# Down projection: activation sums made in the convolution and kept in HBM, 25 groups by seven

## The chip, the cores and the metric

One core of one Trainium2 chip runs the kernel. The metric is device time in microseconds; a lower number is better. The profile names the engines PE (matrix multiply), PEld (its weight loads), DVE (vector), ACT (scalar), POOL (GpSimd) and SP (which issues most DMAs).

## The reference

One transformer block on 256 tokens of width 2048: three attention branches with gates, then a gated feed-forward layer with a short convolution. The change concerns only its last lines (`D_FF` is 5632):

```python
h2 = rms_norm(x, g_ffn[l])
u = causal_depthwise_conv(h2 @ w_up[l], conv_w[l], conv_b[l])
u_gate, u_val = jnp.split(u, 2, axis=-1)
x = x + (jax.nn.silu(u_gate) * u_val) @ w_down[l]
```

## The kernel before

All products keep nearly float32 accuracy by splitting each operand into a high and a low part: ACT casts the raw tile to `hi`, DVE subtracts to get `lo`, and PE adds three products, high by high, low by high and high by low (`three`, lines 1309 to 1311). Of `hi` and `lo` there are four buffers each (`SBUFS`). A cast waits until PE has finished with what lay in the buffer four casts before.

**The up projection** (lines 1219 and 1221) streams 176 weight tiles of 128x1024. Its results go through `conv`, which DVE and ACT work off beside PE: scale, three taps, SiLU, product `g`, and the split of `g` into `aT`, the activations of the down projection, transposed, with high and low part. `conv` takes two feature slices of 128 at a time, 22 such pairs.

**The down projection** multiplies `aT` (44 slices of 128 features) by `w_down` in two halves `nb` of 1024 output columns. A group `p` is a pair of slices `k0 = 2p`, `k1 = 2p+1`, with two halves `t` of the tokens and two halves `n` of the columns: a 2x2 by 2x2 block product. `eight` does it in eight block products (24 matmuls of 128x512). `seven` does it in seven (21 matmuls), by a scheme of Strassen's kind: four of the seven use sums of the weights, `T1` to `T4`, and sums of the activations, `FS1` to `FS4` ("forms"). `PLANS` gives the order in each half; an "e" is a group by eight, an "s" a group by seven. Before, there are 8 and 14 sevens.

Where the sums come from, before:

- Weight sums: `weight_sums` runs during the up projection, one group every seven weight tiles. It loads the four blocks, adds on DVE and stores T4 and T2 to HBM by POOL's queue; for the 12 groups in `ALL_FOUR` it stores T1 and T3 too. In the other 10, `p2` of `seven` makes T1 and T3 by two additions on DVE (lines 1371 and 1372) into a tile of its own.
- Forms: `forms(p)` makes them during the down projection by five DVE instructions from `aT` (lines 1273 to 1277), then splits them by two casts on ACT (1281, 1282) and two subtractions on DVE (1284, 1285). Results lie in `sf` and in parts of `aT` no longer needed.

**What sets the order.** In the down projection the order on each engine is written out: `steps` holds pairs (preparation, use), an eight has two, a seven four (`p0`/`u0` to `p3`/`u3`, of 3, 6, 6 and 6 matmuls); the preparation of step i+2 is issued ahead of the use of step i (`AHEAD`), and `keep` pins it. `after_step` starts generators after a given step; `tick` advances each of at most four by one piece a step. In the trace each engine runs its instructions in that order. SP issues the loads of weights as their buffers (`raw`, `more`) come free. POOL's queue carries the stores of sums, the loads of the residual (`xr`) and half of the results. The tag `junk` has two buffers; `conv`'s scratch, `forms` and `gather` share them.

Of the kernel before, what the change touches and what calls it, by code (L numbers as in the profile page):

```python
# [15 lines left out]
P = 128  # L16
# [32 lines left out]
OUT_SEVENS = 3  # L49
NSEVEN = tuple(plan.count("s") for plan in PLANS)  # L50


@with_exitstack
def hybrid_block(
# [1075 lines left out]
    def conv(ps, f, s):  # L1130
# [20 lines left out]
        if s == 0:  # L1151
            nc.scalar.activation(y, y, AF.Silu)
            ys[f] = y
        else:
            g = ys.pop(f)
            nc.vector.tensor_tensor(g, g, y, ALU.mult)
# [7 lines left out]
            ended.append(f)  # L1164

    ended = []
    made = {}
    asked = [(0, p) for p in range(NSEVEN[0])] + [(1, p) for p in range(NSEVEN[1])]

    def weight_sums(nb, p):  # L1170
# [10 lines left out]
        add = lambda o, i: tc.keep_in_program_order(nc.vector.tensor_tensor(o, o, i, ALU.add))  # L1181
        four = (nb, p) in ALL_FOUR
        add(r[0][:, 0], r[0][:, 1])
        if four:
            add(r[0][:, 1], r[1][:, 1])
        yield 1
        add(r[1][:, 1], r[0][:, 0])
        add(r[1][:, 0], r[1][:, 1])
        made[nb, p] = [dram.tile([P, PIECE], F32, name=f"T{j}_{nb}_{p}") for j in range(1 + four)]
        if four:  # L1190
            nc.gpsimd.dma_start(made[nb, p][1], r[0].rearrange("p b n -> p (b n)"))
        yield 1
# [53 lines left out]
    ov = out[0].rearrange("(t p) d -> p t d", p=P)  # L1246
    FS3, FS1, FS2, FS4 = range(4)
# [8 lines left out]
    def form_of(p, f):  # L1256
        if f == FS4:
            return pieces_of(p)[:, 0, :, 1]
        if p < 10:
            return sf[:, p, f]  # L1260
        return pieces_at(31 - p).rearrange("p k (f l q) -> p (k f) l q", f=2, l=2)[:, f]

    def forms(p):

        flat = aT[:, 2 * p : 2 * p + 3].rearrange("p k s -> p (k s)").bitcast(F32)
        v = flat[:, :1024].rearrange("p (k l t q) -> p k l t q", k=2, l=2, t=NT)
        d = sm.tile([P, 512], F32, tag="junk", bufs=2, name=f"fd_{p}").rearrange("p (f l q) -> p f l q", f=2, l=2)
        r = down_pool().tile([P, 512], F32, tag="fr", bufs=1, name=f"fr_{p}").rearrange("p (f q) -> p f q", f=4)
        g = rbc.rearrange("p (k q) -> p k q", k=2)
        two = flat[:, : 2 * 640].rearrange("p (a b) -> p a b", b=640)[:, :, :512]  # L1270
        two = two.rearrange("p a (l t q) -> p a l t q", l=2, t=NT)[:, :, :, 0]
        tt = nc.vector.tensor_tensor
        keep(tt(d, two, v[:, 0, :, 1].unsqueeze(1).to_broadcast([P, 2, 2, P]), ALU.subtract))
        keep(tt(g, v[:, :, 0, 0], v[:, :, 1, 0], ALU.add))
        keep(tt(r[:, :2], d[:, :, 0], d[:, :, 1], ALU.add))
        keep(nc.vector.scalar_tensor_tensor(r[:, FS2], r[:, FS1], -1.0, g[:, 0], ALU.mult, ALU.subtract))
        keep(tt(r[:, FS4], r[:, FS2], g[:, 1], ALU.add))
        yield
        to = sf[:, p] if p < 10 else form_of(p, slice(0, 3))
        last = form_of(p, FS4)  # L1280
        keep(nc.scalar.copy(to[:, :, 0], r[:, :3]))
        keep(nc.scalar.copy(last[:, 0], r[:, FS4]))
        yield
        keep(tt(to[:, :, 1], r[:, :3], to[:, :, 0].bitcast(F32), ALU.subtract))
        keep(tt(last[:, 1], r[:, FS4], last[:, 0].bitcast(F32), ALU.subtract))

    turn = [0]

    def buffer(name):
        turn[0] += 1  # L1290
        if turn[0] > 10 and turn[0] % 3 == 0:
            return down_pool().tile([P, PIECE], F32, tag="more", bufs=2, name=name)
        return wp.tile([P, PIECE], F32, tag="raw", name=name)

    def load(src, name):
        raw = buffer(f"raw_{name}")
        keep(nc.sync.dma_start(raw[:, : src.shape[1]], src))
        return raw
# [51 lines left out]
    def seven(p, n0, X, Y, first, last):  # L1350
        k0, k1 = 2 * p, 2 * p + 1
        name = f"{n0}_{p}"
        w, raw = {}, {}
        four = (n0 // PIECE, p) in ALL_FOUR

        def p0():
            n = 512 if four else PIECE
            raw[0] = load(dv[:, k0, n0 : n0 + n], f"s{n0}_{k0}")
            (w["00"],) = parts(raw[0][:, :512], f"s{n0}_{k0}")

        def p1():
            raw[1] = load(dv[:, k1, n0 : n0 + PIECE], f"s{n0}_{k1}")
            w["10"], w["11"] = parts(raw[1], f"s{n0}_{k1}")

        def p2():
            raw[2] = load(made[n0 // PIECE, p][0], f"t{name}")
            raw[3] = down_pool().tile([P, PIECE], F32, tag="t13", bufs=2, name=f"t13_{name}")
            if four:
                keep(nc.sync.dma_start(raw[3], made[n0 // PIECE, p][1]))
            else:  # L1370
                keep(nc.vector.tensor_tensor(raw[3][:, :512], raw[0][:, :512], raw[0][:, 512:], ALU.add))
                keep(nc.vector.tensor_tensor(raw[3][:, 512:], raw[0][:, 512:], raw[1][:, 512:], ALU.add))
            w["T4"], w["T2"] = parts(raw[2], f"t42_{name}")

        def p3():
            w["T1"], w["T3"] = parts(raw[3], f"t13_{name}")

        def u0():
            three(Y()[0], *a_of(k0, 0), w["00"], first, last)

        def u1():
            three(X()[0][0], *a_of(k1, 0), w["10"])
            three(X()[0][1], *f_of(p, FS4), w["11"])
# [62 lines left out]

    formed = 0
    after_step = {}
# [4 lines left out]
    for nb, plan in enumerate(PLANS):  # L1453
# [5 lines left out]
        if nb == 0:  # L1459
            at(-1, lambda: start(0))  # L1460
        for i, c in enumerate(plan):
            if c == "s":
                seven(s, n0, X, Y, s == 0, s == ns - 1)
                s += 1
                if s == ns:
                    at(len(steps) - 1, lambda nb=nb: later(gather(nb, banks[nb][1])))
            else:
                eight(straight.pop(0), n0, X, i == 0, i == len(plan) - 1)
                n_done += 1
                if n_done == 4:  # L1470
                    at(len(steps) - 1, lambda nb=nb: residual(nb))
                if formed < ns and n_done >= 4 - 3 * nb:
                    at(len(steps) - 2, lambda p=formed: later(forms(p)))
                    formed += 1
        assert s == ns and not straight and formed >= ns
        at(len(steps) - 1, finish)
# [48 lines left out]
```

## Time and profile before

| | |
|---|---|
| three runs | 1472.62 us median, 1472.32 to 1474.24 |
| profiled execution, first to last instruction | 1469.9 us; the median run lies 2.7 us above it |
| down projection, first to last matmul | 1241.05 to 1465.25 us |
| DVE, ACT, POOL busy over the whole span | 82%, 61%, 5% |
| HBM read, written | 349.70 MB, 37.75 MB |

All times below are microseconds from the start of the span. In the rows of the trace a time stands first and a duration second where the row is one of the timeline; an engine's row in square brackets tells how long it sat idle before and what ended that. Instructions on DVE and ACT overlap a little at their ends, so a row's successor can start before it is over; costs in a row of back-to-back work go by start to start.

### The profile page before, as it was taken

The page shows a single profiled execution, that of the slowest core. Times are in us where ns is not written, and L with a number is a line of the kernel's source. Part 1 is how long each engine was busy: PE and PEld are TensorE (multiplying, and loading weights), DVE is VectorE, ACT ScalarE, POOL GpSimd, SP SyncE. Part 2 cuts the span into 40 slices and gives each one's busy share as a digit, 9 for nine tenths or more (in the row PEclk, how much of TensorE's full clock was granted, in tenths as well). Part 3 has the DMA queues.
Part 4 walks back from the last instruction along what each step waited for, and adds up shares of the span by engine and source line. Part 5 has one row for each costly group of instructions (what it writes and reads, how often), then busy time and mean ns, then how long its engine had stood idle before and what let it go on. Part 6 is the DMA issues. An engine that isn't in the chain of part 4 may idle for free.

```text
span 1469.9 us, 20741 instructions
## 1 busy us (share of the span) xinstructions
PE 1462.8 (100%) x7327; PEld 1233.4 (84%) x7327; DVE 1205.1 (82%) x1617; ACT 895.3 (61%) x1287; POOL 68.8 (5%) x139
## 2 busy tenths in 40 slices
PE   9999999999999999999999999999999999999998
PEld 7888888888878888888888888888888888888887
DVE  5798767766997799888877888788887886998998
ACT  6755454454664466545657667567676777665774
POOL 1000001021000000000000000000000010000000
PEclk9999999999999999999999999999999999999999
DMA  8697898787766576866776888889888895778995
GB/s 295 202 341 260 265 313 270 226 294 267 256 221 204 204 271 247 287 222 237 273 239 218 302 272 276 294 277 310 295 265 273 280 305 190 249 256 286 334 315 191
DMA packets 163463, 388.81 MB, mean 265 GB/s; under 512 B 14016, under 2 KB 22512, under 8 KB 163360
## 3 DMA queue, kind: packets, MB, share of 16 engines
q1 hardware_dynamic: 150960, 345.34, 70.6%
q0 software_dynamic: 11648, 41.10, 7.3%
q8 instruction: 57, 0.93, 0.3%
q10 hardware_dynamic: 752, 1.06, 0.2%
q14 instruction: 46, 0.38, 0.1%
HBM read 349.70 MB, written 37.75 MB: 264 GB/s over the span
## 4 chain that ended last, share of the span: by engine, by line
PE 94%; DVE 3%; DMA 2%; issue 1%; ACT 0%; SPq 0%; DVEq 0%; ACTq 0%
PE u L1219 21%; PE u L1221 10%; PE d L1310 5%; PE d L1309 5%; PE d L1311 5%; PE g_x L769 4%; PE g_x L770 4%; PE g_x L771 4%; PE s L186 2%; PE s L188 2%; PE f L187 2%; PE f L188 2%; PE f L186 2%; PE s L187 2%; PE b L186 2%; PE b L188 2%
## 5 line engine op out<-in xcount | busy, mean ns | idle before, releaser
L1219 PE MATMUL u<-hT,hi_u 128*128 128x512 f32 x1408 | 442.6, 396 | 0.0
L1221 PEld LDWEIGHTS u<-hT,lo_u 128*128 128x128 f32 x1408 | 264.4, 188 | 63.5 <-DVE lo_u L176 1.1
L1221 PE MATMUL u<-hT,lo_u 128*128 128x256 f32 x1408 | 277.0, 278 | 0.7 <-DVE lo_u L176 0.7
L176 DVE TENSOR_TENSOR lo_u<-raw_u,hi_u 128x1024 fp32r<-128x1024 f32 x176 | 213.2, 1220 | 59.8 <-ACT hi_u L175 59.0
L175 ACT CAST hi_u<-raw_u 128x1024 fp32r<-128x1024 f32 x176 | 183.0, 1049 | 107.0 <-PE u L1219 54.6
L1219 PEld LDWEIGHTS u<-hT,hi_u 128*128 128x128 f32 x1408 | 214.5, 189 | 0.1
L764 ACT CAST hi_g<-raw_g 128x1024 fp32r<-128x1024 f32 (+1 forms) x96 | 91.1, 964 | 53.5 <-PE g_x L770 33.4
L765 DVE TENSOR_TENSOR lo_g<-raw_g,hi_g 128x1024 fp32r<-128x1024 f32 (+1 forms) x96 | 105.0, 1116 | 20.9 <-ACT hi_g L764 20.8
L769 PE MATMUL g_x<-hi_g,xT 128*128 128x512 f32 x251 | 98.8, 394 | 0.0
L770 PE MATMUL g_x<-hi_g,xT 128*128 128x512 f32 x251 | 97.7, 389 | 0.0
L771 PE MATMUL g_x<-lo_g,xT 128*128 128x512 f32 x251 | 96.3, 390 | 0.0
L1148 DVE TENSOR_TENSOR y<-y,z 128x512 f32<-128x512 f32 x88 | 60.7, 691 | 24.4 <-ACT z L1147 20.5
L1147 ACT ACTIVATE z<-u,taps 128x256 f32<-128x256 f32 x176 | 74.7, 496 | 0.0
L1309 PE MATMUL d<-hi_d,aT 128*128 128x512 f32 x176 | 68.5, 389 | 0.0
L1310 PE MATMUL d<-hi_d,aT 128*128 128x512 f32 x176 | 68.5, 389 | 0.0
L1311 PE MATMUL d<-lo_d,aT 128*128 128x512 f32 x176 | 68.1, 389 | 0.0
L175 ACT CAST hi_f<-raw_f 128x1024 fp32r<-128x1024 f32 (+1 forms) x40 | 38.6, 968 | 46.6 <-PE f L187 41.9
L186 PE MATMUL s<-hi_s,xT 128*128 128x512 f32 (+1 forms) x160 | 61.9, 387 | 0.0
L175 ACT CAST hi_b<-raw_b 128x1024 fp32r<-128x1024 f32 x32 | 33.6, 1052 | 45.2 <-PE b L187 23.5
L175 ACT CAST hi_s<-raw_s 128x1024 fp32r<-128x1024 f32 (+1 forms) x40 | 38.3, 959 | 36.8 <-PE s L187 29.3
L186 PE MATMUL f<-hi_f,xT 128*128 128x512 f32 (+1 forms) x160 | 60.4, 377 | 0.0
L188 PE MATMUL s<-lo_s,xT 128*128 128x512 f32 (+1 forms) x160 | 59.1, 369 | 0.0
(498 smaller groups left out, 3265.0 us busy)
## 6 DMA issues: line engine op xcount, KB each, us to landing
raw_u<-in_w_up_dram SPq DMA_DIRECT2D x176, 512.0 KB, 5.4
raw_g<-in_w_in_dram SPq DMA_DIRECT2D x86, 512.0 KB, 5.4
T<-r POOLq DMA_DIRECT2D x64, 512.0 KB, 6.1
r<-in_w_down_dram SPq DMA_DIRECT2D x88, 256.0 KB, 5.2
raw_d<-in_w_down_dram SPq DMA_DIRECT2D x44, 512.0 KB, 5.4
raw_f<-in_w_in_dram SPq DMA_DIRECT2D x32, 512.0 KB, 5.5
raw_s<-in_w_in_dram SPq DMA_DIRECT2D x32, 512.0 KB, 5.4
raw_s<-in_w_down_dram SPq DMA_DIRECT2D x32, 512.0 KB, 5.3
```

The source lines that it names most:

```text
L175: pin(nc.scalar.copy(hi[:, :m], raw[:, :m]))
L176: pin(nc.vector.tensor_tensor(lo[:, :m], raw[:, :m], hi[:, :m].bitcast(F32), ALU.subtract))
L186: nc.tensor.matmul(o, lhsT=xh, rhs=wh, start=first, stop=False)
L188: nc.tensor.matmul(o, lhsT=xh, rhs=wl, start=False, stop=last)
L769: nc.tensor.matmul(o, lhsT=a[0], rhs=w[0], start=first, stop=False)
L770: nc.tensor.matmul(o, lhsT=a[1], rhs=w[0], start=False, stop=False)
L771: nc.tensor.matmul(o, lhsT=a[0], rhs=w[1], start=False, stop=last)
L1219: nc.tensor.matmul(ps, lhsT=hi[:, j, c], rhs=hT[:, k + j, :], start=first, stop=False)
L1221: nc.tensor.matmul(ps[:, :S], lhsT=lo[:, j, c], rhs=hT[:, k + j, :S], start=False, stop=last)
L1309: nc.tensor.matmul(o, lhsT=ah, rhs=w[0], start=first, stop=False)
L1310: nc.tensor.matmul(o, lhsT=al, rhs=w[0], start=False, stop=False)
L1311: nc.tensor.matmul(o, lhsT=ah, rhs=w[1], start=False, stop=last)
```

## The change

The unsplit forms (five additions' worth, now three instructions) are made at the end of `conv`, from `g`, for the first 15 pairs of slices, in the tile of `y`, and stored to HBM (`rform`) by POOL. `forms(p)` now loads them back by POOL's queue into a `junk` tile, waits three steps, and splits them as before. There are 25 sevens, 10 and 15. The eight groups in `OWN` have no weight sums in HBM: `p1` of `seven` makes all four by four additions on DVE, in place in the two raw tiles. The other 17 load all four sums from HBM. `weight_sums` is started every nine weight tiles. Of the buffers for raw weights, `more` has four and is used every second time; the tile for T1 and T3 is gone.

```diff
-PLANS = ("eeeee" + "se" * 5 + "sse" + "s" + "eee", "e" + "sse" * 4 + "ssse" + "sssee")
-ALL_FOUR = {(0, 6), (0, 7)} | {(1, p) for p in range(14) if p not in (4, 6, 8, 11)}
+PLANS = ("eee" + "sse" * 5 + "e" + "eee", "e" + "ssse" * 4 + "sss" + "ee")
+OWN = {(0, 1), (0, 3), (0, 5), (0, 7), (0, 9), (1, 3), (1, 7), (1, 11)}
...
+            if f // 2 < NFORM:
+                yield 1
+                unsplit_forms(f // 2, g, y)
...
+    def unsplit_forms(p, g, y):
+        v = g.rearrange("p k (t q) -> p (k t) q", t=NT)
+        r = y.rearrange("p k (t q) -> p (k t) q", t=NT)
+        tt = nc.vector.tensor_tensor
+        tt(r[:, :2], v[:, 0:4:3], v[:, 1:2].to_broadcast([P, 2, P]), ALU.subtract)
+        nc.vector.scalar_tensor_tensor(r[:, FS2], r[:, FS1], -1.0, v[:, 0], ALU.mult, ALU.subtract)
+        tt(r[:, FS4], r[:, FS2], v[:, 2], ALU.add)
+        rforms[p] = dram.tile([P, 512], F32, name=f"rform{p}")
+        nc.gpsimd.dma_start(rforms[p], y.rearrange("p k s -> p (k s)"))
...
-                if asked and n_ticks[0] > 8 and n_ticks[0] % 7 == 2:
+                if asked and n_ticks[0] > 8 and n_ticks[0] % 9 == 2:
...
     def forms(p):
...
+        r = sm.tile([P, 512], F32, tag="junk", bufs=2, name=f"fr_{p}").rearrange("p (f q) -> p f q", f=4)
+        keep(nc.gpsimd.dma_start(r.rearrange("p f q -> p (f q)"), rforms[p]))
+        yield 3
+        to, last = form_of(p, slice(0, 3)), form_of(p, FS4)
         keep(nc.scalar.copy(to[:, :, 0], r[:, :3]))
         keep(nc.scalar.copy(last[:, 0], r[:, FS4]))
         yield
...
-        if turn[0] > 10 and turn[0] % 3 == 0:
-            return down_pool().tile([P, PIECE], F32, tag="more", bufs=2, name=name)
+        if turn[0] > 10 and turn[0] % 2 == 0:
+            return down_pool().tile([P, PIECE], F32, tag="more", bufs=4, name=name)
...
         def p1():
             raw[1] = load(dv[:, k1, n0 : n0 + PIECE], f"s{n0}_{k1}")
             w["10"], w["11"] = parts(raw[1], f"s{n0}_{k1}")
+            if own:
+                add(raw[0][:, :512], raw[0][:, 512:])
+                add(raw[0][:, 512:], raw[1][:, 512:])
+                add(raw[1][:, 512:], raw[0][:, :512])
+                add(raw[1][:, :512], raw[1][:, 512:])
 
         def p2():
...
+            if not own:
+                raw[1] = load(made[n0 // PIECE, p][0], f"t{name}")
+                raw[0] = load(made[n0 // PIECE, p][1], f"t13_{name}")
+            w["T4"], w["T2"] = parts(raw[1], f"t42_{name}")
...
         if nb == 0:
             at(-1, lambda: start(0))
+            for p in range(10):
+                at(p + 1, lambda p=p: later(forms(p)))
         for i, c in enumerate(plan):
             if c == "s":
                 seven(s, n0, X, Y, s == 0, s == ns - 1)
+                if nb and s + 10 < NFORM:
+                    at(len(steps), lambda p=s + 10: later(forms(p)))
```

What the change moves stands best in the engines' own order. First ACT, at the first two groups by seven of the first half and the eight behind them. `hi_s` is the high part of a raw weight, `hi_t42` and `hi_t13` those of the weight sums, `hi_d` that of a weight of a group by eight, `sf` and `aT` from `fr_p` the two copies of form `p`. Before:

```order
L1304 CAST hi_s0_1_12062<-raw_s0_1_12060 128x1024
L1281 CAST sf_11814<-fr_1_12054 128x3x128
L1282 CAST aT_6836<-fr_1_12054 128x128
L1304 CAST hi_t42_0_0_12085<-raw_t0_0_12080 128x1024
L1304 CAST hi_t13_0_0_12094<-t13_0_0_12082 128x1024
L1304 CAST hi_d0_26_12106<-raw_d0_26_12104 128x1024
L1304 CAST hi_d0_27_12118<-raw_d0_27_12116 128x1024
```

In the change, from the second seven's first sum on (the first seven's stand above it):

```order
L1304 CAST hi_t42_0_1_12084<-raw_s0_3_12068 128x1024
L1280 CAST sf_11849<-fr_2_12031 128x3x128
L1281 CAST aT_6836<-fr_2_12031 128x128
L1280 CAST sf_11849<-fr_3_12033 128x3x128
L1281 CAST aT_6836<-fr_3_12033 128x128
L1304 CAST hi_t13_0_1_12095<-raw_s0_2_12049 128x1024
L1280 CAST sf_11849<-fr_4_12047 128x3x128
L1281 CAST aT_6836<-fr_4_12047 128x128
L1304 CAST hi_d0_26_12113<-raw_d0_26_12111 128x1024
L1280 CAST sf_11849<-fr_5_12061 128x3x128
L1281 CAST aT_6836<-fr_5_12061 128x128
L1304 CAST hi_d0_27_12133<-raw_d0_27_12131 128x1024
```

Before, one pair of copies stood in each seven; now pairs 2 to 5 stand between the casts of the second seven and of the eight behind it, pairs 6 and 7 likewise ahead of `hi_t13_0_2`, pair 8 ahead of `hi_s0_6` and pair 9 ahead of `hi_s0_7` of the fourth seven.

Next POOL, whose queue carries the loads of the forms; in brackets the semaphores that an issue waits for (DMASW are landings of earlier transfers of this queue). Before, no such load exists. Now:

```order
L1277 DMA fr_2_12031<-rform2_7878 128x512 [waits DMASW0_49,DMASW5_49,DVE_49,Activation_49]
L1404 DMA xr_0_1_1_12191<-xkeep1_6083 128x512 [waits DMASW6_49]
L1277 DMA fr_3_12033<-rform3_7883 128x512 [waits DMASW1_49,DMASW7_49,DVE_49,Activation_49]
L1277 DMA fr_4_12047<-rform4_8333 128x512 [waits DMASW5_49,DVE_49,Activation_49]
L1277 DMA fr_5_12061<-rform5_8338 128x512 [waits DMASW7_49,DVE_49,Activation_49]
L1277 DMA fr_6_12127<-rform6_8794 128x512 [waits DMASW0_49,DMASW2_49,DVE_49,Activation_49]
```

Each waits for DVE and ACT, since `junk` has two buffers: the load of form p+2 goes out once form p has been split.

Last DVE, in the second seven, a group of `OWN`. Before, a seven that makes T1 and T3 itself (the form's five instructions left out of these rows):

```order
L1305 TENSOR_TENSOR lo_s0_3_12156<-raw_s0_3_12153,hi_s0_3_12155 128x1024
L1371 TENSOR_TENSOR t13_0_1_12175<-raw_s0_2_12128 128x512
L1372 TENSOR_TENSOR t13_0_1_12175<-raw_s0_2_12128,raw_s0_3_12153 128x512
L1305 TENSOR_TENSOR lo_t42_0_1_12179<-raw_t0_1_12173,hi_t42_0_1_12178 128x1024
L1284 TENSOR_TENSOR sf_11814<-fr_2_12147,sf_11814 128x3x128
L1285 TENSOR_TENSOR aT_6836<-fr_2_12147,aT_6836 128x128
L1305 TENSOR_TENSOR lo_t13_0_1_12188<-t13_0_1_12175,hi_t13_0_1_12187 128x1024
```

In the change:

```order
L1305 TENSOR_TENSOR lo_s0_3_12071<-raw_s0_3_12068,hi_s0_3_12070 128x1024
L1355 TENSOR_TENSOR raw_s0_2_12049<-raw_s0_2_12049 128x512
L1355 TENSOR_TENSOR raw_s0_2_12049<-raw_s0_2_12049,raw_s0_3_12068 128x512
L1355 TENSOR_TENSOR raw_s0_3_12068<-raw_s0_3_12068,raw_s0_2_12049 128x512
L1355 TENSOR_TENSOR raw_s0_3_12068<-raw_s0_3_12068 128x512
L1305 TENSOR_TENSOR lo_t42_0_1_12085<-raw_s0_3_12068,hi_t42_0_1_12084 128x1024
L1305 TENSOR_TENSOR lo_t13_0_1_12096<-raw_s0_2_12049,hi_t13_0_1_12095 128x1024
L1283 TENSOR_TENSOR sf_11849<-fr_2_12031,sf_11849 128x3x128
L1284 TENSOR_TENSOR aT_6836<-fr_2_12031,aT_6836 128x128
```

`hi_t42` now reads `raw_s0_3`, so its cast stands behind the low part of the same tile and four additions; before, it read a tile that came from HBM.

More of the change, by code (lines that the diff above doesn't have):

```diff
@@ L1188, in weight_sums @@
         add(r[1][:, 0], r[1][:, 1])
-        made[nb, p] = [dram.tile([P, PIECE], F32, name=f"T{j}_{nb}_{p}") for j in range(1 + four)]
-        if four:
-            nc.gpsimd.dma_start(made[nb, p][1], r[0].rearrange("p b n -> p (b n)"))
+        made[nb, p] = [dram.tile([P, PIECE], F32, name=f"T{j}_{nb}_{p}") for j in range(2)]
+        nc.gpsimd.dma_start(made[nb, p][1], r[0].rearrange("p b n -> p (b n)"))
         yield 1
@@ L1353, in seven @@
         w, raw = {}, {}
-        four = (n0 // PIECE, p) in ALL_FOUR
+        own = (n0 // PIECE, p) in OWN
+        add = lambda o, i: keep(nc.vector.tensor_tensor(o, o, i, ALU.add))
         def p0():
-            n = 512 if four else PIECE
+            n = PIECE if own else 512
             raw[0] = load(dv[:, k0, n0 : n0 + n], f"s{n0}_{k0}")
@@ L1471, in hybrid_block @@
                     at(len(steps) - 1, lambda nb=nb: residual(nb))
[L1472 to L1475, printed above, removed]
+        assert s == ns and not straight
         at(len(steps) - 1, finish)
```

47 lines of the change are left out of this document (11 added, 36 removed).

## The prediction

> **What bounds the kernel now.** I read the page first, then the stages of the second half, then single instructions of the down projection.
>
> ```profile
> PE 1462.8 (100%) x7327; PEld 1233.4 (84%) x7327; DVE 1205.1 (82%) x1617; ACT 895.3 (61%) x1287; POOL 68.8 (5%) x139
> ```
>
> ```profile
> core 0: us, PE busy (x) PEld busy (x) DVE busy (x) ACT busy (x) POOL busy (x), PEclk, DMA share, GB/s
> 900.00:1000.00 100.00, 99.32 (x571) 86.36 (x570) 79.63 (x97) 66.51 (x101) 5.86 (x11) 1.00 0.87 288
> 1138.00:1241.00 103.00, 103.00 (x593) 89.86 (x593) 82.87 (x98) 72.77 (x113) 5.59 (x11) 1.00 0.82 269
> 1270.00:1305.00 35.00, 35.00 (x157) 28.97 (x156) 34.70 (x52) 22.35 (x28) 0.00 (x0) 1.00 0.75 260
> 1355.00:1412.00 57.00, 57.00 (x254) 47.19 (x253) 53.31 (x75) 38.60 (x47) 3.24 (x6) 1.00 0.92 322
> ```
>
> PE never rests in the down projection (the last two rows), and in the up projection (the two above) it lost 0.7 us in one stretch. DVE is at 34.7 of 35 us in one stretch and DMA at 0.92 in another. A busy PE need not be a PE at its pace, so I check that by counting:
>
> ```profile
> 1241.05 0.40 PE L1309 MATMUL d<-hi_d,aT 128*128 128x512 f32 x1
> ...
> 1465.25 0.39 PE L1311 MATMUL d<-lo_d,aT 128*128 128x512 f32 x1
> ```
>
> 22 sevens of 21 and 22 eights of 24 are 990 matmuls; 224.20 us over 989 steps are **0.2267 us** each, the spacing of neighbours too. So PE runs without a gap: every microsecond that a tile is late shows in the end.
>
> How late may a tile be? ACT's rows of two neighbouring sevens:
>
> ```profile
> 1426.28 0.62 ACT L1304 CAST hi_s<-raw_s 128x512 fp32r<-128x512 f32 x1
> 1427.37 1.05 ACT L1304 CAST hi_s<-raw_s 128x1024 fp32r<-128x1024 f32 x1 [0.47 <-PE d L1310]
> 1428.73 1.06 ACT L1304 CAST hi_t<-raw_t 128x1024 fp32r<-128x1024 f32 x1 [0.30 <-PE d L1310]
> 1430.09 1.05 ACT L1304 CAST hi_t<-t 128x1024 fp32r<-128x1024 f32 x1 [0.30 <-PE d L1310]
> ```
>
> The casts come at steps of 1.36 us (six matmuls), each released by PE: with four buffers ACT can't run further ahead. The second starts 0.10 us before the seven in front ends its second step; PE wants this seven's third tile 21 matmuls after that end, 4.86 us after the cast's start. The last, done at 1431.14, is wanted about 1433.6: **the lead is some 2.5 us**.
>
> **The change, part by part.**
>
> *Fewer products.* Three more sevens save 3 matmuls each: 9 x 0.2267 = **-2.0 us**, all on PE's path.
>
> *Up projection.* The 15 forms cost DVE three instructions each, by the rows of this kernel's own forms:
>
> ```profile
> 1274.33 0.42 DVE L1275 TENSOR_TENSOR fr<-fd 128x256 f32<-128x256 f32 x1
> 1274.78 0.29 DVE L1276 SCALAR_TENSOR_TENSOR fr<-fr,rbc 128x128 f32<-128x128 f32 x1
> 1275.11 0.29 DVE L1277 TENSOR_TENSOR fr<-fr,rbc 128x128 f32<-128x128 f32 x1
> ```
>
> That is 1.0 us, 15 in all; 17 groups of four additions instead of 12 of four and 10 of three save 10 x 0.6 = 6. The 9 us more lie beside PE, since DVE idles for a fifth of these stretches: I take 0. The stretch that lost 0.7 us bounds it: -0.7 if that goes, +1.4 if it doubles. The 15 stores on POOL hold only a `y` tile that isn't wanted for another 40 us.
>
> *Sums made in the seven itself.* DVE's rows for its pace, and an addition that needs the one before it:
>
> ```profile
> 1275.32 1.22 DVE L1305 TENSOR_TENSOR lo_s<-raw_s,hi_s 128x1024 fp32r<-128x1024 f32 x1
> 1276.45 0.68 DVE L1371 TENSOR_TENSOR t<-raw_s 128x512 f32<-128x512 f32 x1
> 1277.05 0.68 DVE L1372 TENSOR_TENSOR t<-raw_s,raw_s 128x512 f32<-128x512 f32 x1
> 1277.66 1.22 DVE L1305 TENSOR_TENSOR lo_t<-raw_t,hi_t 128x1024 fp32r<-128x1024 f32 x1
> ...
> 1457.39 0.68 DVE L1411 TENSOR_TENSOR e<-e,d 128x512 f32<-128x512 f32 x1
> 1458.11 0.69 DVE L1413 TENSOR_TENSOR f<-e,d 128x512 f32<-128x512 f32 x1
> ```
>
> Start to start, a low part takes 1.13, a half tile 0.60, a dependent addition 0.72. Before, T4 and T2 came from HBM and their cast waited for a buffer alone. In a group of `OWN` it stands behind cast (1.05), low part (1.13) and four additions (2.88); with its own 1.05 and four hand-overs of about 0.04 that is 6.26 us, against the 4.86 that PE leaves behind another seven: PE waits **1.4**. Behind an eight there is room (33 matmuls, 7.5 us), so group 3 of the second half costs nothing. Seven of the eight stand behind a seven; five (5, 7, 9 of the first half, 7 and 11 of the second) give 5 x 1.4 = **7.0 us**, the other two lie in the next part. Two kinds of work leave DVE (forms, T1 and T3); as PE waits for the chain and not for DVE's total, that gains nothing.
>
> *Forms loaded back.* This is the large one. ACT works in order, and the copies of forms 4 to 9 now stand ahead of casts that PE wants at once. Form p+2 can be loaded only when DVE has split form p, and a load takes (the last such rows of POOL's queue, 256 KB each, then the 512 KB stores of sums in the up projection):
>
> ```profile
> xr<-xkeep POOLq DMA_DIRECT2D x4, 256.0 KB, 6.4
> ...
> DMA to landing us min/median/max: 5.0/6.4/7.3
> ```
>
> ```profile
> DMA to landing us min/median/max: 2.9/6.1/9.3
> ```
>
> The four loads were made beside a busy weight queue. While PE stands still the weights' buffers are full and that queue rests, so I take **L = 5.5**, between their shortest and median; ends 2.9 and 7.3. For the copies:
>
> ```profile
> 1417.18 0.51 ACT L1281 CAST aT<-fr 128x384 fp32r<-128x384 f32 x1 [0.99 <-DVE fr L1276]
> 1417.60 0.29 ACT L1282 CAST aT<-fr 128x128 fp32r<-128x128 f32 x1
> 1417.89 1.06 ACT L1304 CAST hi_t<-raw_t 128x1024 fp32r<-128x1024 f32 x1
> ...
> 1278.79 0.55 DVE L1284 TENSOR_TENSOR sf<-fr,sf 128x384 fp32r<-128x384 f32 x1
> 1279.26 0.28 DVE L1285 TENSOR_TENSOR aT<-fr,aT 128x128 fp32r<-128x128 f32 x1
> ```
>
> Copies 0.71, subtractions about 0.70. Where the path starts:
>
> ```profile
> 1249.00 1.29 DVE L1148 TENSOR_TENSOR y<-y,z 128x512 f32<-128x512 f32 x2
> 1250.20 0.69 DVE L1156 TENSOR_TENSOR y<-y,y 128x512 f32<-128x512 f32 x1
> 1250.81 1.22 DVE L1305 TENSOR_TENSOR lo_d<-raw_d,hi_d 128x1024 fp32r<-128x1024 f32 x1
> ...
> raw_d<-in_w_down_dram SPq DMA_DIRECT2D x38, 512.0 KB, 5.6
> ```
>
> The sixth tile's low part (1250.81 here) gets one product more ahead of it and ends about 1252.9; the tenth load, T1 and T3 of the first seven, takes that tile's buffer and lands 5.6 us later at 1258.5; cast 1.05: DVE starts its low part at **1259.6**. From there, in the order of both engines: to the second seven's T4/T2 cast (low part, form 1's subtractions, half, low part, four additions) 1.13+0.70+0.60+1.13+2.88 = 6.44; that cast, copies of forms 2 and 3, cast of T1/T3 0.96+1.42+1.09 = 3.47; its low part, form 2's subtractions, issue 1.93; **load 4**; copies and the eight's cast 1.80; two low parts and two forms' subtractions 3.76; **load 7**; copies and cast 1.80; low part, form 6's subtractions, issue 1.93; **load 8**; copies, half cast (0.60), copies of form 9, cast 3.11; low part and four additions 4.01; cast 1.09. Together 29.34 + 3L: the fourth seven's third step starts at 1288.9 + 3L. Undisturbed, PE would be there 168 matmuls after 1241.05, at 1279.1. So this costs 9.8 + 3L = **26.3 us** at L = 5.5 (18.5 and 31.7 at the ends).
>
> The Trainium skill (DMA: Bandwidth & Descriptors, section Anatomy of one DMA, the GpSimd path) fits such a transfer by 2.0 us and its bytes at 436 GB/s, an estimate of 2.6 us here; the kernel would then take about 1495 us. No row of this case is that short, and the four of this very size took 5.0 to 7.3.
>
> *DMA in the second half.* 15 sevens load nearly what 14 did; the busiest stretch leaves 8% of 57 us. I take 0, bounds 0 and +3.
>
> Sum: -2.0 + 7.0 + 26.3 = +31.3 on a span of 1469.9; the median run lies 2.7 above that, so 1472.6 + 31.3 = **1504**.
>
> **The rivals.**
>
> *The loads land in time* (0.12). If they ran ahead far enough, copies would wait for nothing and the two other `OWN` groups cost 1.4 too: 7 x 1.4 - 2.0 = +7.8, 1480. For it: POOL is idle. Against: two buffers.
>
> *PE is slower after a long rest* (0.06). The trace holds no gap long enough to show it; the clock stands at 1.00 throughout. My sum has gaps near 7 us. What PE loses inside the path is hidden by the next load; behind the last gap one seven at half pace would add 21 x 0.2267 = 4.8: 1509. The Trainium skill (TensorE: Matmul & The Clock Gate, section on the HAM clock gate) says this: the clock halves after an idle window of about 3.4 us. No run here shows it yet.
>
> *The lead covers it, not slower* (0.04). If tiles lay ready far enough ahead, only -2.0 remains: 1470.6. It decides at the eighth form: PE takes 1.36 us from one blocked cast to the next, the path L + 3.7, so some 8 us of lead are needed where 2.5 are there.
>
> *DMA binds the second half as well* (0.04): its 3 us and the dear end of L, over 1514. *Faster by relief of DVE* (0.02): PE has only 0.7 us to win, with the -2.0 at best 1469.9, hardly beyond measuring.
>
> **How the numbers follow.** The forecast has 0.72: from -2.0+7.0+18.5-0.7 = +22.8 to -2.0+7.0+31.7+1.4+3 = +41.1, 1495 to 1514. The range reaches to the first rival, 1480 to 1514. About 0.2% (2.9 us) can be told from no change: faster 0.02, same 0.04, slower 0.94.
>
> **What would show it.** ACT's copies `sf<-fr` wait for DMA, five us and more at forms 4, 7 and 8; PE has its long gaps there, between 1265 and 1306, none in the up projection, and 1.4 us at each of the five later groups. Wrong: copies that find their data, landings near 2 us, an up projection that ends later than 1241, or a second half above 109 us (483 matmuls) by more than its two gaps.

## The result and the profile after

| | before | after |
|---|---|---|
| time, median of four runs (range) | 1472.82 us (1472.32 to 1474.24) | **1510.53 us** (1508.64 to 1513.19) |
| ratio, 95% interval | | 1.0261 (1.0244 to 1.0278) |
| span of the profiled execution | 1469.9 us | 1506.9 us |
| first and last start of a matmul of the down projection | 1241.05, 1465.25 | 1241.33, 1502.45 |
| between these two | 224.20 us, 990 matmuls | 261.12 us, 981 matmuls |

The change costs 37.7 us; 1504 was predicted, with a range of 1480 to 1514. The profiled executions differ by 37.0 us, and the last row holds 36.9 of them. So the loss lies in the down projection.

The page's line of engines after, and stages of after (time, then busy microseconds of each engine, the granted clock, the DMA share and GB/s, as in the prediction):

```profile
PE 1475.0 (98%) x7318; PEld 1235.2 (82%) x7318; DVE 1201.9 (80%) x1602; ACT 898.1 (60%) x1295; POOL 85.0 (6%) x169
```

```profile
752.00:1238.00 486.00, 486.00 (x2798) 424.16 (x2797) 396.24 (x513) 340.83 (x531) 26.32 (x49) 1.00 0.82 272
1241.00:1270.00 29.00, 24.85 (x107) 19.34 (x106) 21.65 (x30) 18.12 (x32) 4.29 (x8) 0.98 0.74 259
1270.00:1310.00 40.00, 25.58 (x74) 16.84 (x74) 20.59 (x32) 15.85 (x29) 3.23 (x6) 0.76 0.45 151
1310.00:1360.00 50.00, 45.97 (x194) 36.49 (x193) 38.44 (x42) 25.78 (x29) 0.00 (x0) 0.97 0.67 242
1360.00:1470.00 110.00, 107.31 (x472) 87.71 (x470) 90.73 (x104) 65.47 (x79) 6.98 (x13) 1.00 0.80 294
```

PE is still "98%" busy, which says little. The first stage, the up projection, is full. Between 1270 and 1310 every engine rests: PE 14 us, DVE half of the time, and DMA falls to 0.45. When all engines and the queues are idle at once, they wait for each other in a chain. Behind 1310 small losses recur. The granted clock, 1.00 in every stage shown of the kernel before, is 0.76 in the third stage.

ScalarE's timeline of after shows the chain (start, duration, operation, and in brackets how long the engine had idled and for what; the rows between these are left out):

```profile
1268.57 1.04 ACT L1304 CAST hi_t<-raw_s 128x1024 fp32r<-128x1024 f32 x1 [4.14 <-DVE raw_s L1355]
1279.09 0.51 ACT L1280 CAST sf<-fr 128x384 fp32r<-128x384 f32 x1 [7.31 <-DMA fr<-rform]
1287.47 0.52 ACT L1280 CAST sf<-fr 128x384 fp32r<-128x384 f32 x1 [0.33 <-DMA fr<-rform]
1290.99 0.51 ACT L1280 CAST sf<-fr 128x384 fp32r<-128x384 f32 x1 [2.80 <-DMA fr<-rform]
1298.41 0.51 ACT L1280 CAST sf<-fr 128x384 fp32r<-128x384 f32 x1 [5.76 <-DMA fr<-rform]
1301.13 0.51 ACT L1280 CAST sf<-fr 128x384 fp32r<-128x384 f32 x1 [1.49 <-DMA fr<-rform]
1306.93 2.00 ACT L1304 CAST hi_t<-raw_s 128x1024 fp32r<-128x1024 f32 x2 [4.15 <-DVE raw_s L1355]
```

The rows of line 1280 are the copies of forms 4, 6, 7, 8 and 9: ahead of each of the five, ScalarE idles until the load has landed. On POOL's queue these loads were issued at:

```profile
1274.23 1.21 POOL L1277 DMA_DIRECT2D fr<-rform  x2 [10.50 <-DVE aT L1284]
...
1285.01 0.54 POOL L1277 DMA_DIRECT2D fr<-rform  x1 [1.27 <-DVE aT L1284]
1295.11 0.54 POOL L1277 DMA_DIRECT2D fr<-rform  x1 [9.56 <-DVE aT L1284]
1298.27 0.55 POOL L1277 DMA_DIRECT2D fr<-rform  x1 [2.62 <-issue]
```

Forms 4, 7 and 8 wait for line 1284, VectorE's last use of the buffer two forms earlier, and are used 4.86, 5.98 and 3.30 us behind their issue. TensorE's timeline shows what that does to the matmuls:

```profile
1269.66 0.79 PE L1309 MATMUL d<-hi_t,sf 128*128 128x512 f32 x1 [2.74 <-ACT hi_t L1304]
...
1280.80 0.80 PE L1309 MATMUL d<-hi_d,aT 128*128 128x512 f32 x1 [5.63 <-ACT hi_d L1304]
...
1299.69 0.79 PE L1309 MATMUL d<-hi_s,aT 128*128 128x512 f32 x1 [4.54 <-ACT hi_s L1304]
1300.28 0.63 PE L1310 MATMUL d<-hi_s,aT 128*128 128x512 f32 x1
1300.71 0.63 PE L1311 MATMUL d<-lo_s,aT 128*128 128x512 f32 x1
1302.83 0.80 PE L1309 MATMUL d<-hi_s,aT 128*128 128x512 f32 x1 [1.50 <-ACT hi_s L1304]
...
1308.03 0.50 PE L1309 MATMUL d<-hi_t,sf 128*128 128x512 f32 x1 [1.86 <-ACT hi_t L1304]
...
1310.37 0.63 PE L1309 MATMUL d<-hi_d,aT 128*128 128x512 f32 x1
1310.80 0.63 PE L1310 MATMUL d<-hi_d,aT 128*128 128x512 f32 x1
...
1313.19 0.40 PE L1310 MATMUL d<-hi_d,aT 128*128 128x512 f32 x1
```

A gap here is the distance of two starts less the pace of 0.2267 us. There are five long ones: 2.91 us (the row at 1269.66), 6.03 (1280.80), 4.70 (1299.69), 1.90 (1302.83) and 2.26 (1308.03). Behind them the matmuls start 0.43 us apart, not 0.23, for 3 to 5 us. From 1313 on there are five more gaps, of 1.50 or 1.51 us each, at the third steps of the groups 5, 7 and 9 of the first half (1326.28, 1342.98, 1359.65) and 7 and 11 of the second (1442.96, 1469.18). At group 7 of the first half TensorE waits for ScalarE's cast, and that cast had waited for VectorE's four additions (line 1355):

```profile
1341.88 2.00 ACT L1304 CAST hi_t<-raw_s 128x1024 fp32r<-128x1024 f32 x2 [4.14 <-DVE raw_s L1355]
1342.98 0.50 PE L1309 MATMUL d<-hi_t,sf 128*128 128x512 f32 x1 [1.34 <-ACT hi_t L1304]
```

### The profile page after: what moved, and what is told of

Read it like the earlier page. It is cut to its first block, busy times and chain, and to the rows that moved or that the text cites. A ratio compares the mean times of both kernels' runs of the same rounds, so it can differ in the third digit from the quotient of the medians.

```text
span 1506.9 us, 20777 instructions
## 1 busy us (share of the span) xinstructions
PE 1475.0 (98%) x7318; PEld 1235.2 (82%) x7318; DVE 1201.9 (80%) x1602; ACT 898.1 (60%) x1295; POOL 85.0 (6%) x169
## 4 chain that ended last, share of the span: by engine, by line
PE 90%; DVE 4%; DMA 2%; ACT 2%; issue 1%; DVEq 0%; ACTq 0%; SPq 0%; POOL 0%; POOLq 0%
PE u L1233 22%; PE u L1235 11%; PE d L1309 4%; PE g_x L770 4%; PE g_x L771 4%; PE g_x L772 4%; PE d L1310 4%; PE d L1311 4%; PE s L187 2%; PE s L189 2%; PE f L187 2%; PE f L189 2%; PE f L188 2%; PE s L188 2%; PE b L189 2%; PE b L188 2%
## 5 line engine op out<-in xcount | busy, mean ns | idle before, releaser
L1149 DVE TENSOR_TENSOR y<-y,z 128x512 f32<-128x512 f32 x88 | 60.8, 691 | 26.3 <-ACT z L1148 22.8
L1309 PE MATMUL d<-hi_d,aT 128*128 128x512 f32 x152 | 60.8, 400 | 5.6 <-ACT hi_d L1304 5.6
L1310 PE MATMUL d<-hi_d,aT 128*128 128x512 f32 x152 | 60.1, 396 | 0.0
L1305 DVE TENSOR_TENSOR lo_d<-raw_d,hi_d 128x1024 fp32r<-128x1024 f32 x38 | 45.4, 1221 | 17.4 <-ACT hi_d L1304 17.3
```

Of the source, the lines that this page charges most:

```text
L1309: nc.tensor.matmul(o, lhsT=ah, rhs=w[0], start=first, stop=False)
L1310: nc.tensor.matmul(o, lhsT=al, rhs=w[0], start=False, stop=False)
```

## The experiments

The theory was that the loss has two parts: the copies that stand in ScalarE's order behind loads only just issued (26 us and more), and the chain of four additions in a group with own sums (1.5 us each). Rivals were VectorE's work as a whole, late weight loads, and TensorE's slow stretches. Differences below are against the kernel before in the same series (1471.72 us median for the first four runs, 1471.96 for the next four, 1471.71 for the last two). "Down" is the time from the first to the last start of a down projection matmul in the profiled execution, 261.12 after.

**Forms spread.** In the first half a group's forms are asked for at most eight steps ahead of it.

```diff
-            for p in range(10):
-                at(p + 1, lambda p=p: later(forms(p)))
...
+                if nb == 0:
+                    at(max(1, len(steps) - 8), lambda p=s: later(forms(p)))
                 seven(s, n0, X, Y, s == 0, s == ns - 1)
```

> One thing is changed: in the first half the forms of a group are loaded at most eight steps ahead of that group, not one group per step from step 1 on; the same loads, copies, subtractions and matmuls are issued. Theory A (the copies that wait behind just-issued form loads hold ScalarE and through it the weight parts): the gaps of 2.91, 6.03, 4.70, 1.90 and 2.26 us between 1265 and 1309 and the 0.43 us matmuls behind them go, about 24 to 29 us; in their place the own sums of the first half, which those gaps had hidden in the second and fourth group by seven, are seen in all five own groups at 1.5 us each, so +3, and up to 4 us stay at the first form. Sum: 1510.5 - 29 + 3 to 1510.5 - 24 + 7, so 1483 to 1494 us. Rival B (VectorE's own sums and the low parts, not the form loads, make the gaps): the long gaps stay near 1265 to 1309, 1503 to 1511 us. Rival C (late loads of the weights raw_s and raw_d, 6.5 us median landing, make them): moving the forms takes 1 to 3 us off, 1507 to 1510 us.

1490.39 us, +18.7, ratio 1.0129 (1.0112 to 1.0146); down 240.37. The same work is done, and 20.7 us of the down projection are gone. ScalarE's timeline of this run, two copies and a cast from it (the rows between are left out):

```profile
1272.03 0.51 ACT L1280 CAST sf<-fr 128x384 fp32r<-128x384 f32 x1
1278.38 0.51 ACT L1280 CAST sf<-fr 128x384 fp32r<-128x384 f32 x1
1287.75 2.00 ACT L1304 CAST hi_t<-raw_s 128x1024 fp32r<-128x1024 f32 x2 [4.51 <-DVE raw_s L1355]
```

No copy waits, though the loads take longer (median 6.5 us from issue to landing, 4.8 after). So not their length cost the time but where their copies stood. What is left are mostly the own sums: 2.89 us at the second group, where two casts had also waited 1.18 and 0.63 us for weight loads, 1.88 at each of the four others of the first half (the theory had 1.5), and 0.41, 1.94 and 1.51 in the second half. One stretch of 0.43 us matmuls stays, behind the 2.89. This is theory A. The rival of late weight loads falls as the cause of the long gaps, since moving the forms alone removed them.

**Own sums behind a pair by eight.** Only the table changes.

```diff
-OWN = {(0, 1), (0, 3), (0, 5), (0, 7), (0, 9), (1, 3), (1, 7), (1, 11)}
+OWN = {(0, 0), (0, 2), (0, 4), (0, 6), (0, 8), (1, 3), (1, 6), (1, 9)}
```

> Only the choice of the eight groups that make their own weight sums is changed: in each case one that stands directly behind a pair of steps by eight, so that two more steps of matmuls cover the four additions and the low part; which groups load made sums changes with it, the number of every operation is the same. Theory A (own sums cost a chain of 6.26 us against 4.86 us of matmuls, once per own group, and nothing else): the five gaps of 1.50 us at 1326, 1343, 1360, 1443 and 1469 go or shrink to at most 0.5 us each, the form-load gaps in the first half stay within 3 us of what they are: 1510.5 - 7.5 to 1510.5 - 5, so 1503 to 1506 us (down to 1501 if the additions also leave the first half's held-up stretch). Rival B (the 1.5 us come from the DVE or the DMA being short over the whole half, not from the place of the group): gaps of the same sum move to the new own groups, 1509 to 1512 us. Rival C (own groups with their four additions are also what delays the early groups): more than 12 us go, under 1498 us.

1500.41 us, +28.7, ratio 1.0199 (1.0184 to 1.0214); down 254.02, 7.1 less than after. Between 1310 and 1400 no gap is left; in the second half 0.27, 1.35 and 0.43 us stay. The form loads still hold the first half up:

```profile
1280.33 0.51 ACT L1280 CAST sf<-fr 128x384 fp32r<-128x384 f32 x1 [6.71 <-DMA fr<-rform]
...
1300.75 0.51 ACT L1280 CAST sf<-fr 128x384 fp32r<-128x384 f32 x1 [7.18 <-DMA fr<-rform]
```

The two parts are separate, and this one has the size that the theory gives it: five gaps of 7.5 us in all become 2.05 us, though the 1.35 is more than the 0.5 that it allows a group. The time is 2.6 us under the theory's main range and 0.6 under the lowest value that it names.

**Both** edits above.

> Both edits at once: the forms of the first half loaded at most eight steps ahead of their group, and each own-sum group directly behind a pair of steps by eight. Theory A (form loads about 26 to 29 us and own sums 7 x 1.5 us are the whole loss and add up): what is left is a wait of 3 to 5 us at the first form, 0.2 to 0.6 us at each of eight own groups, less 2.0 us for nine matmuls fewer: 1473 to 1481 us, so from as fast as the kernel before to 0.6% slower. Rival B (something else that the change added, such as the DMA traffic of the forms or the up projection, costs 5 us or more): 1485 us or above. Rival C (with the waits gone the nine matmuls and the relief of VectorE show): under 1471 us.

1485.95 us, +14.2, ratio 1.0096 (1.0081 to 1.0111); down 235.70. This misses theory A by 5 us and lies in the range of rival B, which has something else cost 5 us or more: the parts don't quite add up (20.7 + 7.1 singly, 25.4 together). Left are 6.5 us in seven gaps between 1261 and 1283, 0.65 us at each later own group of the first half (0.43 to 0.46 and 0.23), and 2.00 at 1415. There was a third part that I hadn't seen; the next runs look for it.

**TensorE kept awake**, on the changed kernel. Matmuls by zero stand ahead of those that wait in the long gaps. There were 68 of them (10, 24, 18, 8, 8), not the 75 of the expectation.

```diff
+    ZEROS = {12: 10, 14: 24, 20: 18, 21: 8, 22: 8}
...
+        for _ in range(ZEROS.get(i, 0)):
+            keep(nc.tensor.matmul(banks[0][0][0][0][:, :384], lhsT=idle[:, :P], rhs=idle, start=False, stop=False))
```

> The changed kernel with 75 matmuls of 128x384 by weights and data of zero put ahead of the matmuls that wait in the long gaps of the first half (10, 24, 18, 15 and 8 of them, about 0.17 us each at full pace, less than each gap); they add zero to an open accumulator, and everything else stands where it stood. Theory A (TensorE runs at half pace, 0.43 us a matmul, for some 4 us behind each long rest, and that lies on the path only behind the last gap): the 0.43 us rows between 1270 and 1313 go, the gaps begin later by what the slow matmuls had taken, and the end moves by the slow stretch behind the last gap alone: 1.5 to 2.5 us off, 1508 to 1509 us. Rival B (the slow stretches lie on the path behind each of the four gaps): 4 to 8 us off, 1502.5 to 1506.5 us. Rival C (the 0.43 us spacing isn't due to rest but to weight parts arriving late): the rows stay at 0.43 us, 1510 to 1512 us.

1509.69 us, +38.0, ratio 1.0260 (1.0244 to 1.0275), not to be told from after; down 260.66. TensorE's timeline of this run, behind the last gap:

```profile
1308.99 0.50 PE L1309 MATMUL d<-hi_t,sf 128*128 128x512 f32 x1 [1.40 <-ACT hi_t L1304]
...
1311.46 0.39 PE L1309 MATMUL d<-hi_d,aT 128*128 128x512 f32 x1
1311.70 0.39 PE L1311 MATMUL d<-lo_t,sf 128*128 128x512 f32 x1
...
1312.60 0.39 PE L1310 MATMUL d<-hi_d,aT 128*128 128x512 f32 x1
```

Fifteen steps behind the gap (to 1312.60 here, to 1313.19 after) take 3.61 us against 5.16: 1.55 us less, so the slow pace there comes from the rest, and rival C falls. Rival B falls as well: nothing like 4 us is gained. Of the 1.55 only 0.46 show in the down projection, since the blocked step came 0.2 us later and another gap, of 0.68 us at 1417, is in this execution and not in the other. One stretch of 0.43 us rows stayed, behind a rest of 3.29 us that the zeros didn't fill. The size of theory A is read from the rows, not from the time, which lies between the ranges of A and C.

**First group from HBM**, on top of both edits.

```diff
-OWN = {(0, 0), (0, 2), (0, 4), (0, 6), (0, 8), (1, 3), (1, 6), (1, 9)}
+OWN = {(0, 2), (0, 4), (0, 6), (0, 8), (1, 3), (1, 6), (1, 9), (1, 12)}
```

> As the run with both edits, but the first group of the first half takes its sums from HBM and a group of the second half (its thirteenth) makes its own in its place, so that no additions stand in the stretch in which VectorE still has the convolution's tail. Theory A (the gaps of 1.0, 0.5, 0.4, 1.8, 0.7 and 1.9 us between 1261 and 1283 in the run with both edits come from the four additions behind the convolution's tail): 3 to 5 us of those 6.5 go, 9 to 11 us above the kernel before, 1481 to 1483 us. Rival B (they come from loads that land late there): they stay within 1 us, 13 to 15 us above the kernel before, 1485 to 1487 us.

1483.85 us, +11.9, ratio 1.0075 (1.0061 to 1.0089); down 234.93. Of the gaps between 1261 and 1283, 4.2 us of the 6.5 stay. The time lies between the two ranges, but the trace says what most of the rest is. Six gaps, 3.2 us, stand between 1261 and 1275, where the DMA queues are full and one cast after the other idles for a weight load:

```profile
1262.00:1275.00 13.00, 10.79 (x40) 6.48 (x39) 7.94 (x9) 7.63 (x10) 0.66 (x2) 1.00 1.03 404
```

```profile
1269.35 1.05 ACT L1304 CAST hi_t<-raw_t 128x1024 fp32r<-128x1024 f32 x1 [1.40 <-DMA raw_t<-T]
1271.82 1.05 ACT L1304 CAST hi_d<-raw_d 128x1024 fp32r<-128x1024 f32 x1 [1.42 <-DMA raw_d<-in_w_down_dram]
```

That is rival B for this part: the weight loads issued between 1253 and 1273 land 8.6 to 12.4 us after their issue (medians by tile), against 5.6 to 5.9 in the kernel before.

**Two additions earlier.** The additions that need no low part move ahead of it.

```diff
+            if own:
+                add(raw[0][:, :512], raw[0][:, 512:])
+                add(raw[0][:, 512:], raw[1][:, 512:])
             w["10"], w["11"] = parts(raw[1], f"s{n0}_{k1}")
             if own:
-                add(raw[0][:, :512], raw[0][:, 512:])
-                add(raw[0][:, 512:], raw[1][:, 512:])
                 add(raw[1][:, 512:], raw[0][:, :512])
```

> As the run before it in this list (first group from HBM), and in each own group the two additions that need no weight part are put ahead of the second weight part's low part instead of behind it, so two additions of 0.7 us leave the chain behind that low part; the number of operations is the same. Theory A (an own group behind a pair by eight still loses about 0.65 us because VectorE has nearly no idle time in the first half: per three groups some 14.5 us of work beside 15.0 us of matmuls): nothing changes, within 1 us of that run. Rival B (the length of the chain behind the low part makes the loss): the small gaps of 0.4 and 0.2 us at each own group go, 2 to 3 us less than that run.

1481.65 us, +9.7, ratio 1.0060 (1.0048 to 1.0073); down 233.68. The gaps at the own groups of the first half are no smaller, 0.57 and 0.23 us (0.45 and 0.23 before); what is gained lies in the second half (0.97 and 1.63 us near 1394 and 1415 there, one gap of 0.91 here). The medians differ by 2.2 us, as rival B has it, but not for its reason: at the first half's own groups the chain's length isn't it. In the second half a shorter chain may have helped; one profile of each can't say. VectorE's timeline of this run, from one own group's sums to the next one's:

```profile
1280.71 1.23 DVE L1305 TENSOR_TENSOR lo_t<-raw_s,hi_t 128x1024 fp32r<-128x1024 f32 x1 [1.19 <-ACT hi_t L1304]
1282.28 1.23 DVE L1305 TENSOR_TENSOR lo_t<-raw_s,hi_t 128x1024 fp32r<-128x1024 f32 x1 [0.34 <-ACT hi_t L1304]
1283.43 0.55 DVE L1283 TENSOR_TENSOR sf<-fr,sf 128x384 fp32r<-128x384 f32 x1
...
1295.08 0.69 DVE L1355 TENSOR_TENSOR raw_s<-raw_s 128x512 f32<-128x512 f32 x1
1296.96 1.23 DVE L1305 TENSOR_TENSOR lo_t<-raw_s,hi_t 128x1024 fp32r<-128x1024 f32 x1 [1.19 <-ACT hi_t L1304]
```

A turn (two groups by seven, one pair by eight) takes VectorE 16.25 us, of which it idles 1.19 + 0.34, both times for a cast that had waited for VectorE's own sums. The other 14.7 us are work without a pause. TensorE needs 66 x 0.2267 = 15.0 us a turn, so each turn loses 1.3 us, 0.80 in the two gaps and the rest in steps of 0.11 us or less. This says that VectorE's round, not one group's chain, sets the pace here; the run with six own groups tests it.

**Groups by seven one pair later**, on top of that.

```diff
-PLANS = ("eee" + "sse" * 5 + "e" + "eee", "e" + "ssse" * 4 + "sss" + "ee")
+PLANS = ("eeee" + "sse" * 5 + "eee", "e" + "ssse" * 4 + "sss" + "ee")
```

> As the run with early additions, with the order of the first half changed from three pairs by eight, five times (two groups by seven, one pair by eight), four pairs by eight, to four, five times, three: all groups by seven of the first half start one pair by eight (5.4 us of matmuls) later. Theory A (what is left at the first two groups is the convolution's tail and the first form loads, both tied to a time and not to the group): it is covered by the pair that now stands ahead, 1 to 3 us less than the run with early additions. Rival B (what is left stands at the groups wherever they are): no change, within 0.7 us.

1478.99 us, +7.0, ratio 1.0043 (1.0029 to 1.0056); down 230.35, 3.3 less. Between 1261 and 1275, 1.1 us of gaps are left. What stood there is tied to the time, as theory A says, but it isn't the convolution's tail itself, whose last instruction starts at 1256.20 in the run before. The trace shows the stretch of full queues in its place: the DMA share from 1262 to 1275 is 1.03 here too, and the pair by eight that now stands ahead covers most of the wait.

**Two additions on GpSimd.** On top of that again, the first two additions of an own group:

```diff
             if own:
-                add(raw[0][:, :512], raw[0][:, 512:])
-                add(raw[0][:, 512:], raw[1][:, 512:])
+                pool_add(raw[0][:, :512], raw[0][:, 512:])
+                pool_add(raw[0][:, 512:], raw[1][:, 512:])
```

where `pool_add` is the same `tensor_tensor` on `nc.gpsimd`.

> As the run with the later groups, but two of the four additions of each own group are made by GpSimd, which has little else to do there; no trace so far shows an addition on GpSimd, so its time is open. Theory A (VectorE's throughput makes the small gaps at the own groups, 1.3 us of its work leave each): the gaps of 0.4 and 0.2 us at the first half's own groups go, 1.5 to 3 us less than the run with the later groups, so 3 to 7 us above the kernel before. Rival B (GpSimd's addition takes over 2 us, or holds VectorE up while it runs, and stands in the chain itself): each own group loses 1 us or more, 4 to 10 us more than the run with the later groups.

1486.86 us, +14.9, ratio 1.0102 (1.0088 to 1.0116); down 237.87. GpSimd's groups of instructions in this run (busy us, mean ns, idle before):

```profile
L1356 POOL TENSOR_TENSOR raw_s<-raw_s,raw_s 128x512 f32<-128x512 f32 x8 | 14.6, 1830 | 0.6
L1356 POOL TENSOR_TENSOR raw_s<-raw_s 128x512 f32<-128x512 f32 x8 | 12.9, 1608 | 69.1 <-DVE lo_s L1305 69.1
```

On the mean 1.6 and 1.8 us where VectorE takes 0.7. Singly they take 1.28 to 1.30 or 2.14 to 2.16 us, one short and one long in each pair; what makes the long one is open. In a turn of the first half VectorE idles 2.55 us for them. The relief is spent in a longer chain, as rival B has it, and the run says nothing on A.

**Six own groups**, on top of the later groups and the early additions.

```diff
-OWN = {(0, 2), (0, 4), (0, 6), (0, 8), (1, 3), (1, 6), (1, 9), (1, 12)}
+OWN = {(0, 4), (0, 8), (1, 3), (1, 6), (1, 9), (1, 12)}
```

> As the run with the later groups, but six groups make their own sums and not eight: two in the first half (fifth and ninth) and four in the second (fourth, seventh, tenth, thirteenth); nineteen take them from HBM, two more sets of sums being made in the up projection. Theory A (VectorE's throughput makes the 0.57 and 0.24 us gaps at an own group in every turn of two groups by seven and one pair by eight; with an own group in every second turn VectorE catches up in between): the gaps go at the two that are left too, not only at the two taken away, so 2 to 4 us less than that run and 3 to 5 us above the kernel before: 1475 to 1477 us. Rival B (each own group pays by itself, for the place that its additions have in the order): two groups keep their 0.8 us, two go: 1.6 us less at most. Rival C (two more sets of sums lengthen the up projection, by 1 us or more each): the down projection starts later and the time is that of the run with the later groups or above it.

1474.51 us (1472.44 to 1478.31), +2.8, ratio 1.0022 (1.0012 to 1.0032); down 224.40. The gaps at *both* own groups left in the first half are gone, as theory A says and rival B does not; what stays there is some 0.4 us a group, in steps of 0.11 us or less. The time is 0.5 us under the theory's range. The stages of this run:

```profile
1275.00:1310.00 35.00, 35.00 (x154) 28.31 (x153) 30.19 (x37) 24.00 (x33) 2.70 (x5) 1.00 0.86 330
1310.00:1360.00 50.00, 50.00 (x221) 40.80 (x220) 42.04 (x53) 27.87 (x33) 3.58 (x7) 1.00 0.78 290
```

PE counts as busy all the way from 1275 to 1360. Two more sets of sums in the up projection cost nothing that shows: the down projection starts at 1241.56, inside the 1240.0 to 1243.6 of the other runs.

**Later forms in the second half**, on top of that. Forms 10 to 14 are loaded behind the eighth to twelfth group by seven, not the first to fifth.

```diff
-                if nb and s + 10 < NFORM:
-                    at(len(steps), lambda p=s + 10: later(forms(p)))
+                if nb and 10 <= s + 3 < NFORM:
+                    at(len(steps), lambda p=s + 3: later(forms(p)))
```

> As the run with six own groups, but the five forms that the second half still loads are loaded behind its eighth to twelfth group by seven and not behind its first to fifth, where VectorE also gathers and writes the first half's results. Theory A (the gap of about 1.2 us near 1410 is VectorE's backlog from the gathering and these subtractions, five times 0.7 us): it goes, 0.5 to 1.5 us less than the run with six own groups, near 1474 to 1476 us, with the kernel before or within 0.3% of it. Rival B (the backlog only moves to the later groups): no change, within 0.7 us.

1475.96 us, +4.2, ratio 1.0031 (1.0019 to 1.0042); down 225.80, 1.4 more. Of the gap near 1410 only 0.36 us had been left with six own groups; that goes, and gaps of 0.22 and 0.54 us come in its place. One of its eight executions took 8404 us; without it the median is 1475.54 us, 1.0 above the run with six own groups, and the two intervals overlap. Theory A's gain isn't there; the gap moves, as rival B has it.

No version beat the kernel before. The best one, with six own groups, does nine matmuls (2.0 us) less than the kernel before and needs as long between the first and the last (224.40 and 224.20); its time is 0.22% longer (0.12% to 0.32%).

## Why the prediction held, and where it was short

The mechanism was right: the two parts named are the loss, in their places, and undoing either one takes its part away. The forecast was 6.5 us short. Step by step, in the profiled executions:

| term | predicted | measured |
|---|---|---|
| nine matmuls fewer | -2.0 | -2.0 (980 x 0.2267 against 989) |
| up projection | 0 (-0.7 to +1.4) | +0.3 (first matmul 1241.33 for 1241.05); +0.9 on the mean of eleven changed profiles |
| forms loaded back, to the fourth seven's third step | +26.3 | +28.6 (1308.03 less 1241.33 + 168 x 0.2267) |
| half pace behind the last gap | 0, as a rival 4.8 | +1.8 (5.16 us for 15 steps) |
| own sums, five groups | +7.0 | +7.5 (1.50 each) |
| DMA in the second half | 0 | 0 (two gaps of 1.51, no other) |
| not placed, many steps of 0.02 to 0.1 | | +1.0 |
| sum | +31.3 | +37.2, with the start |

- **The loads.** L = 5.5 was the part that I doubted most, and the three on the path took 14.1 us together for 16.5. It was the work between them that was mis-sized: the second group's cast began at 1268.57 for a predicted 1266.04, behind three weight loads that landed 6.1, 7.6 and 8.7 us after their issue and not 5.6; form 9 came late as well (1.49 us), since POOL issued it 2.62 us late, for which the trace names no cause; small hand-overs gave 1.0. Two errors of opposite sign hid each other, which made L look better chosen than it was: that this part came out within 2.3 us was in part luck.
- **The clock.** The rival "PE is slower after a long rest" was given 0.06 and is what happened, with 1.8 us for 4.8: the slow stretch is some 3 us long, not a whole group, and what is slow inside the path is mostly covered by the next load, as the step said. The Trainium skill (TensorE: Matmul & The Clock Gate, Part 1) has the clock halved after an idle window of about 3.4 us, and 426.7 ns between matmuls of 512 columns. The trace agrees on the spacing, 0.43 us; on the time it differs: a rest of 2.89 us was enough in the run with forms spread, and none up to 2.0 us was in the run with both edits. The last slow stretch here follows a rest of 2.26 us that came directly behind slow matmuls.
- **Own sums.** 1.50 for 1.4. Seven such groups paid when the form loads stopped hiding two of them, as the rival "loads land in time" has it; it put the time at 1480 and the run with forms spread came to 1490: there the seven gaps came to 13.9 us for 9.8 (2.89, 1.94, 1.51 and four of 1.88), the stretch at half pace added 1.4, and the down projection began 2.1 us later than after.
- **A step that was wrong, without weight here:** "as PE waits for the chain and not for DVE's total, that gains nothing", and that behind a pair by eight there is room. Once the loads are out of the way, an own group in every turn of the first half costs 1.2 to 1.3 us a turn behind a pair by eight as well, 0.65 to 0.8 of it in gaps, and shortening the chain doesn't help; one in every second turn costs some 0.4. There VectorE's round is the limit.
- **The lead.** That 2.5 us of lead can't cover the loads held for one load per step. With each form asked for eight steps ahead of its group no copy waited.
- **A term that the sum lacked.** The part "DMA in the second half" looked for full queues in the wrong place. With the form loads out of the way they were full at the start of the down projection (DMA share 1.03 from 1262 to 1275 in the runs with the first group from HBM, with early additions and with later groups). In the changed kernel late loads are in the 2.5 us by which the second group's cast came late.

Open: what delays POOL's issue of form 9, why so many loads meet between 1253 and 1275, and where 2 of the 2.8 us of the best version lie, as its profiled execution was its fastest (1472.44).

## What to carry to other kernels

A tile that is fetched back through two buffers runs at the pace of load plus use, and its copy in an in-order engine makes everything behind it wait: spread such loads to the rate at which they are used before looking at their length. When all engines and the DMA rest at once, look for a chain, and expect TensorE to come back slowly behind it. Before extra work goes to one engine in each turn of a loop, add up that engine's whole turn, hand-overs too, against TensorE's: the place of the work matters only while the turn has room.

## What the runs showed of the hardware

- TensorE's pace halves behind a rest: 0.43 us per 128x512 fp32r matmul for 3 to 5 us, seen behind rests of 2.89 to 6.66 us, and behind one of 2.26 us that followed longer ones; it returns by itself while the matmuls run on.
- Loads of 256 KB on POOL's queue landed 2.8 to 8.4 us after issue in one kernel (median 4.8 after, 6.5 with forms spread); stores of that size on ScalarE's queue at the end took 2.5.
- With the queues full (DMA share 1.03, 404 GB/s, the run with the first group from HBM) weight loads of 512 KB landed 8.6 to 12.4 us after issue by the medians, against 5.6 to 5.9 in the kernel before in that stretch.
- An addition of 128x512 float32 takes GpSimd 1.28 to 1.30 us or 2.14 to 2.16 us (means 1.6 and 1.8 by operands), VectorE 0.68.
